# Setting up triangles between the steps of a state, and a modulation product on column quarters

## The chip, the cores and the metric

The kernel runs on one core of a Trainium2 chip. The metric is the device time of one execution in microseconds (us), lower is better. The engines are TensorE (PE; its weight loads are shown apart as PEld), VectorE (DVE), ScalarE (ACT), GpSimd (POOL) and SyncE (SP), which here issues all transfers between the device's memory and the cores' memory in one queue.

## The reference, cut to what matters

Two layers of a hybrid trunk over 2304 tokens (256 of context, 2048 latent) of 1024 channels. Each layer modulates a layer norm, projects it, runs three branches (a gated DeltaNet in both directions, a neighbourhood attention, a gated linear attention) and projects back.

```python
def ada_modulation(cond, w_mod, b_mod):
    h = (jax.nn.silu(cond) @ w_mod + b_mod)[..., None, :]
    return jnp.split(h, 3, axis=-1)
...
    amat = jnp.eye(c, dtype=F32) + lmat
    rhs = jnp.concatenate([v * beta[..., None], kb * jnp.exp(g)[..., None]], -1)
    sol = lax.linalg.triangular_solve(amat, rhs, left_side=True, lower=True, unit_diagonal=True)
...
    def step(s, inp):
        qk_i, qd_i, kd_i, u_i, w_i, gl_i = inp
        v_new = u_i - jnp.einsum('bhck,bhkv->bhcv', w_i, s)
        o = jnp.einsum('bhck,bhkv->bhcv', qd_i, s) + jnp.einsum('bhij,bhjv->bhiv', qk_i, v_new)
        s = s * gl_i[..., None, None] + jnp.einsum('bhck,bhcv->bhkv', kd_i, v_new)
        return s, o
```

The modulation has two rows (one for the latent tokens, one for the context) and 3072 columns per layer. The DeltaNet has four heads and two directions; its state is stepped chunk by chunk, and each chunk needs the inverse of a unit triangular matrix.

## The kernel before, in words

The program is written out in Python. A scheduler orders the instructions of each engine by priority, which is the order in which the program emits them: what is emitted first goes first when it is ready, and later work fills the gaps. The order is then fixed, and each engine runs its queue in order. Projections (`Dense`, L190) are three fp32r products per pair of blocks.

`stage_mod` (L90) computes the modulation in parts of 512 columns. For each part it loads eight tiles of weights of 128 x 512 (L102), multiplies them by the conditioning's two columns into a 2 x 512 output (L104), adds the bias (L105) and, for the first four parts, transposes the result into `modT` (L111, L112); the last two parts are the gate and go to `GT`. It runs in three places: at the very start (parts 0 to 3 of layer 0), inside layer 0 before the convolution of the DeltaNet's first two heads (parts 4 and 5 of layer 0 and 0 to 3 of layer 1), and at the same place in layer 1 (parts 4 and 5).

The DeltaNet works on chunks of 128 tokens, 18 of them; 3 chunks make a group. Heads go in pairs (`hp`, two of them), and the triangles of a pair are set up in three batches of two groups (`BATCHES`, six in all). For a batch there are three pieces of work:

- `prep` (L831): six chunks; each loads `kq` and `gb` (256 KB each), makes a product `pk` on TensorE (L849), and on DVE and ACT the triangle X and the matrix A (L853 to L860). The 32 x 32 diagonal blocks go out to device memory.
- `diagonal` (L879), with `invert` (L902): inverts 96 x 32-sized blocks on DVE: 30 rounds of one multiplication (L913) and one addition (L914).
- `solve` (L887), with `assemble` (L916): puts the inverse of the 128 x 128 triangles together with small TensorE products in five stages (L930, L936, L945, L956, L962).

`scan` (L966) steps the state: step n of both directions side by side. `step` (L978) has stages divided by `yield`: the product pk with the state (L999), R on DVE (L1003), pv (L1010), v on ACT (L1013), pd (L1017), the new state S on DVE (L1022), then the output po (L1030, L1032), which from the second visit of a chunk on is added to what the first visit stored (a load L1035, an addition L1036, a store L1040). A pair of heads has 18 steps, so a layer has 36, and they form one chain through the state.

The first batch is set up in `start`, between the convolutions of the two pairs. `run` emits the rest as a generator. Before its first `yield` stand prep(1), prep(2) and solve(0); then the layer emits the dense product for z (`dn.run(Wz, ...)`), and after it, up to the second `yield`, diagonal(1), solve(1), six steps, prep(3) and so on; each diagonal is emitted right before its solve. Then follow the attention of its first pair of heads (`na.pair`), the rest of `run`, and the attention of the second pair. So z's products have priority over all steps, and attention fills what the steps leave.

## Time and profile before

| | before |
|---|---|
| runs shown, median (lowest to highest) | 3989.75 us (3979.24 to 4000.7), 3 runs |
| profiled execution, its own time | 3995.01 us |
| its span, first to last instruction | 3992.9 us |
| mean granted TensorE clock | 0.913 |
| TensorE / DVE / ACT / POOL busy | 3626.0 / 2521.8 / 1660.0 / 810.2 us |
| bytes moved by DMA | 787.57 MB |

The profile comes from one execution of the program. A busy share is an average over stages that have different limits; a stage's own limit is read from a window of time, and a wait from the instruction that ended it.

### The profile page before, as it was taken

What the parts mean: (1) busy time and instruction counts of PE and PEld (TensorE: products, weight loads), DVE (VectorE), ACT (ScalarE), POOL (GpSimd) and SP (SyncE); (2) the same over time, 40 slices, a digit from 0 to 9 for tenths busy, and PEclk for the clock granted to TensorE, in tenths of its full rate; (3) what the DMA queues carried; (4) which work ended last, traced back from release to release, by engine and by line L of the source; (5) the groups of instructions that cost most, each with busy time, mean ns of one, the idle gap of its engine ahead of it and who ended that gap; (6) DMA issues with size and microseconds to landing.
All of it is one profiled execution on the core that took longest, in us unless ns stands there. A gap on an engine that the chain in (4) does not pass through costs nothing.

```text
span 3992.9 us, 77074 instructions
## 1 busy us (share of the span) xinstructions
PE 3626.0 (91%) x27262; PEld 3113.1 (78%) x27262; DVE 2521.8 (63%) x7471; ACT 1660.0 (42%) x4387; POOL 810.2 (20%) x1182
## 2 busy tenths in 40 slices
PE   7999998899989999897898999999999898989788
PEld 3777787579977888896676778887998788879676
DVE  5465462668975676356875556527798766753587
ACT  4533231335433454446545333213454244545342
POOL 0121111210101332221232211112111132331133
PEclk8988988899999998898898888899999998988899
DMA  9843435876687876666647443268776887775753
GB/s 312 280 147 105 133 112 169 245 232 201 205 276 219 246 229 189 187 196 214 203 132 232 152 147 115 100 210 251 215 232 201 285 228 205 228 217 150 219 160 111
DMA packets 756088, 787.57 MB, mean 197 GB/s; under 512 B 190207, under 2 KB 665207, under 8 KB 755703
## 3 DMA queue, kind: packets, MB, share of 16 engines
q1 hardware_dynamic: 755702, 782.64, 63.6%
q8 instruction: 216, 3.54, 0.4%
q14 instruction: 170, 1.38, 0.1%
HBM read 548.41 MB, written 234.03 MB: 196 GB/s over the span
## 4 chain that ended last, share of the span: by engine, by line
PE 55%; DMA 19%; DVE 16%; ACT 4%; issue 3%; SPq 2%; POOL 0%; DVEq 0%; ACTq 0%; POOLq 0%
PE p L190 29%; DMA mm<-MS 3%; PE p L1245 3%; DMA gb<-GR 2%; PE p L104 2%; DMA kk<-KK 2%; DMA raw<-in_w_in 1%; PE py L190 1%; PE po L1030 1%; PE pk L999 1%; PE pv L1010 1%; DMA oa<-OA 1%; PE pd L1017 1%; PE pt L1236 1%; DVE y L1374 1%
## 5 line engine op out<-in xcount | busy, mean ns | idle before, releaser
L190 PE MATMUL p<-mm,wh 128*128 128x384 f32 (+1 forms) x3648 | 1004.0, 354 | 67.2 <-DMA mm<-MS 21.4
L190 PEld LDWEIGHTS p<-mm,wh 128*128 128x128 f32 (+1 forms) x3648 | 667.8, 192 | 133.7 <-DMA mm<-MS 36.9
L190 PE MATMUL p<-mm,wl 128*128 128x384 f32 (+1 forms) x1824 | 635.1, 350 | 1.8 <-DVE wl L182 1.8
L190 PE MATMUL p<-wh,mm 128*128 128x512 f32 (+1 forms) x1696 | 570.5, 409 | 14.5 <-DMA mm<-MS 4.9
L190 PEld LDWEIGHTS p<-wh,mm 128*128 128x128 f32 x1696 | 329.1, 197 | 92.0 <-DMA mm<-MS 8.4
L649 DVE SCALAR_TENSOR_TENSOR acc<-pre,cw,acc 128x384 f32<-128x384 f32 (+1 forms) x576 | 351.8, 629 | 39.2 <-ACT acc L647 35.8
L190 PEld LDWEIGHTS p<-mm,wl 128*128 128x128 f32 (+1 forms) x1824 | 348.9, 191 | 22.8 <-issue 14.6
L190 PE MATMUL p<-wl,mm 128*128 128x512 f32 (+1 forms) x848 | 341.5, 403 | 4.3 <-DVE wl L182 4.3
L190 PE MATMUL py<-wh,mh 128*128 128x512 f32 x544 | 221.7, 410 | 17.1 <-ACT mh L1360 13.2
L190 PE MATMUL py<-wh,ml 128*128 128x512 f32 x544 | 213.9, 405 | 8.7 <-DVE ml L1361 8.7
L190 PE MATMUL py<-wl,mh 128*128 128x512 f32 x544 | 217.8, 402 | 0.0
L190 PEld LDWEIGHTS p<-wl,mm 128*128 128x128 f32 x848 | 166.5, 196 | 38.5 <-DVE wl L182 4.8
L992 POOL TENSOR_TENSOR kd<-kk,eD 128x256 f32<-128x256 f32 x144 | 90.4, 628 | 476.4 <-DMA kk<-KK 225.6
L1224 ACT ACTIVATE w<-w,mn 128x696 f32<-128x696 f32 (+2 forms) x136 | 112.9, 830 | 143.9 <-DVE mn L1221 142.6
L1383 POOL TENSOR_TENSOR y<-y,g 128x1024 f32<-128x1024 f32 x32 | 77.5, 2423 | 416.0 <-ACT y L1382 416.0
L639 POOL COPY pre<-pre 128x4 f32<-128x4 f32 x120 | 75.0, 627 | 416.4 <-DVE acc L649 244.1
L913 DVE TENSOR_TENSOR tmp<-M 96x30 f32<-96x30 f32 (+4 forms) x360 | 127.1, 353 | 27.7 <-issue 11.3
L1245 PE MATMUL p<-v,wl 120*128 120x64 f32 (+1 forms) x960 | 141.1, 286 | 0.0
L853 DVE SCALAR_TENSOR_TENSOR gb<-gb,Gt,mats 128x128 f32<-128x128 f32 x288 | 86.7, 358 | 83.0 <-DMA gb<-GR 82.8
L1261 DVE SCALAR_TENSOR_TENSOR zt<-zt,p 128x256 f32<-128x256 f32 (+1 forms) x102 | 51.4, 506 | 138.8 <-ACT zt L1260 131.9
L190 PEld LDWEIGHTS py<-wh,mh 128*128 128x128 f32 x544 | 106.4, 196 | 41.4 <-ACT mh L1360 16.1
L914 DVE TENSOR_TENSOR M<-M,tmp 96x30 f32<-96x30 f32 (+4 forms) x360 | 130.4, 362 | 6.1
(307 smaller groups left out, 8021.8 us busy)
## 6 DMA issues: line engine op xcount, KB each, us to landing
mm<-MS SPq DMA_DIRECT2D x384, 384.0 KB
kk<-KK SPq DMA_DIRECT2D x144, 512.0 KB
MS<-mm SPq DMA_DIRECT2D x96, 384.0 KB
raw<-in_w_in SPq DMA_DIRECT2D x104, 256.0 KB
w<-in_w_mod SPq DMA_DIRECT2D x96, 256.0 KB
M<-m SPq DMA_DIRECT2D x36, 512.0 KB
mm<-M SPq DMA_DIRECT2D x96, 192.0 KB
KK<-kq SPq DMA_DIRECT2D x96, 192.0 KB
```

The costliest lines, as they stand in the source:

```text
L104: nc.tensor.matmul(p, e.cc[:, k + j], w[:, j], start=k + j == 0, stop=k + j == KD - 1)
L190: e.nc.tensor.matmul(p, x(k), y(k), start=n == 0, stop=n == 3 * KD - 1)
L639: nc.gpsimd.tensor_copy(pre[:, 0:4], pre[:, m:m + 4])
L649: nc.vector.scalar_tensor_tensor(acc[:, :n], pre[:, k:k + n], w(kind, k), acc[:, :n], op0=ALU.mult, op1=ALU.add)
L853: nc.vector.scalar_tensor_tensor(E[:, d, h], gb[:, d, h], self.G[:, d, c, h0 + h:h0 + h + 1], e.mats[:, 1 + d], op0=ALU.subtract, op1=ALU.min)
L913: nc.vector.tensor_tensor(tv, col, row, op=ALU.mult)
L914: nc.vector.tensor_tensor(o, o, tv, op=ALU.add)
L992: nc.gpsimd.tensor_tensor(kd, kv[:, :, 0], self.eD[:, d, c, h0:h0 + 2].unsqueeze(2).to_broadcast([128, 2, 128]), op=ALU.mult)
L1224: nc.scalar.activation(w[:, a, 0:256 + nk], w[:, a, 0:256 + nk], AF.Exp, bias=m[:, a:a + 1], scale=-1.0, accum_out=sm[:, a:a + 1])
L1245: nc.tensor.matmul(p[:, a], l, r, start=j == 0, stop=j == len(parts) - 1)
L1261: nc.vector.scalar_tensor_tensor(th[:, :n], th[:, :n], 1.0, z, op0=ALU.add, op1=ALU.mult)
L1383: eng.tensor_tensor(y[:, s], y[:, s], self.g[:, 0, s], op=ALU.mult)
```

## The change

Two parts. `stage_mod` takes all its parts at once: for each of the eight slices of the contraction it loads tiles of 128 x 1024 weights (two parts), and the products of part i write to partitions 32i to 32i + 1 of one output bank, with the tile position (0, 32i), each part on its own quarter of the array's columns. Four bias additions follow, and four full transposes serve all parts.

The DeltaNet's `prep` and `diagonal` become generators with a `yield` after each chunk and each of the 30 rounds. `scan` takes such generators and, after each stage of a step but the first, runs `share // 6` of their parts, where `share` is 48 divided by the number of steps, rounded up: two parts for three steps, one for six. prep(2) now comes after the first three steps, and steps 0 to 2, diagonal(1) and prep(2) are emitted before the z product.

```diff
-def stage_mod(e, pool, ps, tag, tt, bufs, w_mod, b_mod, modT, GT, parts, step):
+def stage_mod(e, pool, ps, tag, tt, bufs, w_mod, b_mod, modT, GT, parts):
...
-        p = ps.tile([2, 512], F32, tag=tag, name="p")
-        for k in range(0, KD, step):
-            w = pool.tile([128, step, 512], F32, tag="wm", name="w", bufs=bufs)
-            nc.sync.dma_start(w, w4[:, k:k + step, s])
-            for j in range(step):
-                nc.tensor.matmul(p, e.cc[:, k + j], w[:, j], start=k + j == 0, stop=k + j == KD - 1)
-        nc.vector.tensor_tensor(b, b, p, op=ALU.add)
...
+    n0, n = parts[0], len(parts)
+    b = pool.tile([128, 512], F32, tag="bm", name="b", bufs=1)
+    nc.gpsimd.memset(b, 0.0)
+    for i, x in enumerate(parts):
+        nc.sync.dma_start(b[32 * i:32 * i + 2], b_mod[512 * x:512 * x + 512].partition_broadcast(2))
+    p = ps.tile([128, 512], F32, tag=tag, name="p")
+    for k in range(KD):
+        for i0 in range(0, n, 2):
+            w = pool.tile([128, 2, 512], F32, tag="wm", name="w", bufs=bufs)
+            nc.sync.dma_start(w, w4[:, k, 512 * (n0 + i0):512 * (n0 + i0) + 1024].rearrange("p (i c) -> p i c", i=2))
+            for i in range(i0, i0 + 2):
+                nc.tensor.matmul(p[32 * i:32 * i + 2], e.cc[:, k], w[:, i - i0], start=k == 0, stop=k == KD - 1, tile_position=(0, 32 * i))
+    for i in range(n):
+        r = slice(32 * i, 32 * i + 2)
+        nc.vector.tensor_tensor(b[r], b[r], p[r], op=ALU.add)
...
-        prep(1)
-        prep(2)
+        run = lambda *g: [None for x in g for _ in x]
+        run(prep(1))
         solve(0)
+        self.scan(self.st[0], range(3), diag(1))
+        run(prep(2))
         yield
-        for k in range(1, 6):
-            solve(k)
-            if k % 3:
-                self.scan(self.st[k // 3], range(6 * (k % 3) - 6, 6 * (k % 3)))
-            else:
-                self.scan(self.st[k // 3 - 1], range(12, 18))
-            prep(k + 2)
-            if k == 3:
-                yield
-        self.scan(self.st[1], range(12, 18))
+        solve(1)
+        self.scan(self.st[0], range(3, 6), diag(2))
+        solve(2)
+        self.scan(self.st[0], range(6, 12), prep(3), diag(3))
+        self.scan(self.st[0], range(12, 18), prep(4), diag(4))
+        yield
+        solve(3)
+        self.scan(self.st[1], range(3), prep(5))
+        solve(4)
+        self.scan(self.st[1], range(3, 6), diag(5))
+        solve(5)
+        self.scan(self.st[1], range(6, 18))
         yield
...
-    def scan(self, s, steps):
+    def scan(self, s, steps, *work):
+
         nc = self.e.nc
+        parts = (x for w in work for x in w)
+        share = -(-48 // len(steps))
...
-            for _ in zip(*both):
-                pass
+            for i, _ in enumerate(zip(*both)):
+                if i:
+                    for _ in range(share // 6):
+                        next(parts, None)
+        for _ in parts:
+            pass
```

At the start of layer 0 the order of emission changes too: the first block's loads of x come first, then one `stage_mod` of four parts with six buffers of 1024 columns in the place of eleven of 512; at the other two places two buffers in the place of four.

What the scheduler made of it, at three places. On TensorE at the second place of the modulation (L190, L198 after, is the projection's product; L104, L107 after, the modulation's), before:

```order
L104 MATMUL p<-w,cc 2x512
L190 MATMUL p<-mm,wl 128x384
L190 MATMUL p<-mm,wh 128x384
L104 MATMUL p<-w,cc 2x512
L190 MATMUL p<-mm,wh 128x384
L190 MATMUL p<-mm,wl 128x384
L190 MATMUL p<-mm,wh 128x384
L104 MATMUL p<-w,cc 2x512
```

and after:

```order
L198 MATMUL p<-mm,wh 128x384
L107 MATMUL p<-w,cc 2x512 x2
L198 MATMUL p<-mm,wh 128x384
L198 MATMUL p<-mm,wl 128x384
L198 MATMUL p<-mm,wh 128x384 x2
L198 MATMUL p<-mm,wl 128x384
L198 MATMUL p<-mm,wh 128x384
L107 MATMUL p<-w,cc 2x512 x2
```

Single products between the projection's became pairs.

On TensorE at the second step of the state in layer 0 (pk, pv, pd, po as above; L930 to L962 are solve), before:

```order
L956 MATMUL pz_13121<-t_13107,X 64x64 x6
L962 MATMUL px_13130<-X,z_13119 64x64 x6
L999 MATMUL pk<-S_13304,kk 128x128 x2
L1010 MATMUL pv<-R,X 128x128 x2
L962 MATMUL px_13138<-X,z_13128 64x64 x6
L930 MATMUL pz<-x_13012,X 32x32 x6
L930 MATMUL pz<-x_13011,X 32x32 x6
L1010 MATMUL pv<-R,X 128x128 x2
L1017 MATMUL pd<-v,kd 128x128 x2
```

and after (L1024, L1035, L1042 are pk, pv, pd; L980 solve; L864 prep; L198 the z product):

```order
L980 MATMUL px_12045<-X,z_12034 64x64 x6
L1024 MATMUL pk<-S_12102,kk 128x128 x2
L1035 MATMUL pv<-R,X 128x128 x2
L198 MATMUL p<-wh,mm 128x512 x2
L198 MATMUL p<-wl,mm 128x512
L198 MATMUL p<-wh,mm 128x512 x2
L198 MATMUL p<-wl,mm 128x512
L198 MATMUL p<-wh,mm 128x512 x2
L198 MATMUL p<-wl,mm 128x512
L198 MATMUL p<-wh,mm 128x512
L980 MATMUL px_12053<-X,z_12043 64x64 x6
L864 MATMUL pk<-kq 128x256 x2
```

Products of z moved in between the stages of the first steps. At the other end of layer 0, the last step and what follows it, before (L1229, L1236, L1245 are attention):

```order
L1010 MATMUL pv<-R,X 128x128 x2
L1229 MATMUL pt<-ident,w 128x128 x2
L1010 MATMUL pv<-R,X 128x128 x2
L1236 MATMUL pt<-ident,w 120x128 x2
L1236 MATMUL pt<-ident,w 80x128
L1017 MATMUL pd<-v,kd 128x128 x2
L1229 MATMUL pt<-ident,w 128x128 x2
L1017 MATMUL pd<-v,kd 128x128 x2
```

and after:

```order
L1024 MATMUL pk<-S_18390,kk 128x128 x2
L1024 MATMUL pk<-S_18393,kk 128x128 x2
L1035 MATMUL pv<-R,X 128x128 x4
L1042 MATMUL pd<-v,kd 128x128 x4
L1055 MATMUL po<-v,A 128x128
L1057 MATMUL po<-S_18390,kk 128x128
```

The last three steps of layer 0 have no attention beside them any more; in layer 1 they had none before either.

## Rows read from the trace of the kernel before

**Rows 1.** The page: busy time of each engine; the chain by engine.

```profile
PE 3626.0 (91%) x27262; PEld 3113.1 (78%) x27262; DVE 2521.8 (63%) x7471; ACT 1660.0 (42%) x4387; POOL 810.2 (20%) x1182
...
PE 55%; DMA 19%; DVE 16%; ACT 4%; issue 3%; SPq 2%; POOL 0%; DVEq 0%; ACTq 0%; POOLq 0%
```

**Rows 2.** Windows: span; us busy (count) of PE, PEld, DVE, ACT, POOL; clock; DMA share; GB/s.

```profile
0.00:45.00 45.00, 32.66 (x81) 6.14 (x81) 16.02 (x45) 5.05 (x10) 0.71 (x6) 1.00 0.94 307
715.00:870.00 155.00, 152.75 (x676) 101.63 (x677) 96.48 (x232) 51.97 (x131) 36.27 (x50) 0.98 0.88 254
1120.00:1220.00 100.00, 85.72 (x446) 67.81 (x445) 74.44 (x263) 30.42 (x82) 10.88 (x27) 0.88 0.99 320
1280.00:1340.00 60.00, 51.41 (x530) 45.82 (x529) 27.25 (x87) 23.85 (x68) 22.25 (x53) 0.91 0.95 255
1340.00:1690.00 350.00, 321.66 (x3118) 296.20 (x3118) 207.50 (x677) 174.22 (x479) 95.23 (x200) 0.89 0.72 206
1690.00:1790.00 100.00, 97.45 (x824) 94.65 (x823) 51.77 (x164) 53.99 (x150) 26.13 (x43) 1.00 0.68 205
2730.00:2780.00 50.00, 49.02 (x209) 31.50 (x210) 46.05 (x95) 21.02 (x47) 17.59 (x28) 0.97 0.97 279
3080.00:3180.00 100.00, 84.41 (x455) 66.23 (x454) 67.77 (x240) 30.36 (x81) 11.24 (x28) 0.89 1.01 331
```

**Rows 3.** TensorE around one product of the modulation (start, us); line L104 altogether.

```profile
754.13 1.02 PE L104 MATMUL p<-w,cc 128*2 128x512 f32 x2
...
755.08 0.45 PE L190 MATMUL p<-mm,wl 128*128 128x384 f32 x1
...
L104 PE MATMUL p<-w,cc x192: 591/592/1057, 9.4 to 2772.1; 128*2 128x512 f32 x192
```

**Rows 4.** TensorE where outputs lie in two halves (L486) and four quarters (L533).

```profile
600.55 0.27 PE L486 MATMUL pA<-a 32*64 32x64 f32 x2
...
629.60 0.39 PE L190 MATMUL p<-wl,mm 128*128 128x512 f32 x1
...
629.91 0.43 PE L533 MATMUL pS<-v,kd 128*32 128x64 f32 x16
...
630.27 0.74 PE L190 MATMUL p<-wh,mm 128*128 128x512 f32 x2
```

**Rows 5.** The chain, 0 to 50 us, in order of time (start, us, what).

```profile
30.20 5.23 DMA w<-in_w_mod
...
37.72 6.18 PE p L104 x14
...
43.92 0.67 DVE b L105
```

**Rows 6.** DVE waiting for gb: group, 1120 to 1220 us; total, times, longest, 1120 to 1800.

```profile
L853 DVE SCALAR_TENSOR_TENSOR gb<-gb,Gt,mats 128x128 f32<-128x128 f32 x51 | 14.5, 345 | 16.7 <-DMA gb<-GR 16.7
...
DVE gb L853 <- DMA gb<-GR: 44.7, 16, 7.0
```

**Rows 7.** The chain in late steps of layer 1, without attention.

```profile
3701.56 5.57 DMA OA<-o
...
3707.19 3.01 DMA o<-OA
...
3743.51 0.22 PE po L1030 x2
```

**Rows 8.** Groups of the whole span: one half of the rounds of inversion.

```profile
L914 DVE TENSOR_TENSOR M<-M,tmp 96x30 f32<-96x30 f32 (+4 forms) x360 | 130.4, 362 | 6.1
```

**Rows 9.** TensorE at pv of steps 3 and 6, and of three late ones, layer 0.

```profile
1298.53 0.71 PE L1010 MATMUL pv<-R,X 128*128 128x128 f32 x4
...
1337.47 0.71 PE L1010 MATMUL pv<-R,X 128*128 128x128 f32 x4
...
1754.37 1.05 PE L1010 MATMUL pv<-R,X 128*128 128x128 f32 x8
...
1775.37 1.05 PE L1010 MATMUL pv<-R,X 128*128 128x128 f32 x8
```

More of the change, by code (lines that the diff above doesn't have):

```diff
@@ new lines, in stage_mod @@
+    for i in range(n):
+        r = slice(32 * i, 32 * i + 2)
+        nc.vector.tensor_tensor(b[r], b[r], p[r], op=ALU.add)
+    if n0 >= 4:
+        for i in range(n):
+            nc.sync.dma_start(GT[:, 512 * (n0 - 4 + i):512 * (n0 - 3 + i)], b[32 * i:32 * i + 2])
+        return
+    pt = ps.tile([128, 4, 128], F32, tag=tt, name="pt")
+    for j in range(4):
+        nc.tensor.transpose(pt[:, j], b[:, j * 128:(j + 1) * 128], e.ident)
+    for i in range(n):
+        m = modT[:, 4 * (n0 + i):4 * (n0 + i) + 4]
+        nc.vector.tensor_scalar(m, pt[:, :, 32 * i:32 * i + 2], float(n0 + i >= 2), None, op0=ALU.add)
@@ L766, in start @@
         ax = lambda: [P.tile([128, 3, 2, 128], F32, tag=t, name=t) for t in "AX"]
-        self.XD[0] = self.prep(s, b, P, ps, "dn", ax)
-        self.diagonal(P, *self.XD[0])
+        for _ in self.prep(s, b, P, ps, "dn", ax, 0):
+            pass
+        for _ in self.diagonal(P, *self.XD[0]):
+            pass
     def weights(self, hp):
@@ L784, in prep, with diag @@
         def prep(k):
-            if k < len(self.BATCHES):
-                hp, b = self.BATCHES[k]
-                self.XD[k] = self.prep(self.st[hp], b, self.P1, self.ps, "pp", self.ax)
+            hp, b = self.BATCHES[k]
+            yield from self.prep(self.st[hp], b, self.P1, self.ps, "pp", self.ax, k)
+        def diag(k):
+            yield from self.diagonal(self.PM, *self.XD[k])
         def solve(k):
             hp, b = self.BATCHES[k]
-            if k:
-                self.diagonal(self.PM, *self.XD[k])
             self.solve(self.st[hp], b, *self.XD.pop(k))
@@ L829, in store, with prep @@
         self.e.nc.sync.dma_start(far["AX".index(t)], x.rearrange("p c h t -> p (c h t)"))
-    def prep(self, s, batch, P, ps, tag, ax):
+    def prep(self, s, batch, P, ps, tag, ax, key):
         e, nc = self.e, self.e.nc
@@ L860, in prep @@
                     nc.vector.tensor_tensor(A[d][:, ci], pk[:, :, 1], E[:, d], op=ALU.mult)
+                yield
             for d in range(2):
@@ L876, in prep @@
             nc.sync.dma_start(LD[b].rearrange("u j i -> j u i"), xd[32 * b:32 * b + 32].rearrange("p g u i -> p (g u) i"))
-        return n, LD, XD
+        self.XD[key] = n, LD, XD
+        yield
     def diagonal(self, P, n, LD, XD):
@@ L883, in diagonal @@
         nc.sync.dma_start(M, LD.rearrange("b u j i -> (b u) j i"))
-        self.invert(P, M, n)
+        yield from self.invert(P, M, n)
         nc.sync.dma_start(XD.rearrange("b u j i -> (b u) j i"), M)
@@ L914, in invert @@
             nc.vector.tensor_tensor(o, o, tv, op=ALU.add)
+            yield
     def assemble(self, X, d, xc, xt, i):
@@ L1428, in layer @@
                 p1 = stage_p1(e, P, ps, xsrc, layers[0].modT, M)
-                for n in (range(2), range(2, 4)):
-                    stage_mod(e, P, ps, "pa", "pm", 11, i["w_mod"][0], i["b_mod"][0], layers[0].modT, GT, n, 1)
-                    next(p1, None)
+                next(p1)
+                stage_mod(e, P, ps, "pa", "pm", 6, i["w_mod"][0], i["b_mod"][0], layers[0].modT, GT, range(4))
+                next(p1, None)
         def cbc(p, t):
@@ L1471, in layer @@
                                 if j < DEPTH:
-                                    stage_mod(e, P1, ps, "dn", "dn", 4, i["w_mod"][j], i["b_mod"][j], layers[j].modT, layers[j].GT, n, 1)
+                                    stage_mod(e, P1, ps, "dn", "dn", 2, i["w_mod"][j], i["b_mod"][j], layers[j].modT, layers[j].GT, n)
                             dn.run(W, gdn.conv(P, psh, 0) + gdn.conv(P, psh, 1), [], bufs=6, raws=4)
```

12 lines of the change are left out of this document (1 added, 11 removed).

## The prediction

> **What bounds the kernel now.** Start with the busy shares and the engines of the chain that ended last [rows 1]: TensorE (PE) is busy 91% of the span and carries 55% of the chain, DMA carries 19%, VectorE (DVE) 16%. So TensorE's instructions are the first currency: what leaves its queue counts where it has no gaps, and a wait counts where TensorE has nothing else to do. The stretches [rows 2] split that. From 715 to 870 us, where the modulation of the next layer runs between the convolution's products, TensorE is busy 152.75 of 155 us and DMA 0.88. At 2730 to 2780, the same place of layer 1, TensorE is full, but so are DVE (46.05 of 50) and DMA (0.97). From 1120 to 1220 and from 3080 to 3180, where triangles are set up before the state's steps, DMA is full (0.99 and 1.01) and TensorE idles 14.3 and 15.6 us. From 1690 to 1790, with attention between the steps, TensorE is full again. The first 45 us are a race of the weight transfers and the modulation's products.
>
> **Modulation on column quarters, second place (715 to 870 us).** One product of two rows is two instructions, since fp32 takes two passes; the row at 754.13 and the next one's start at 755.08 give 0.95 us from entry to exit [rows 3]. 48 of them take 48 x 0.95 = 45.6 us. After the change two products whose outputs lie in different quarters stand next to each other. That such pairs run at once is in the trace: two instructions on two 64-column halves take 0.27 us together, no more than one alone, and after 16 instructions on four quarters, which start at 629.91, the next full product starts at 630.27, 0.36 us later [rows 4]. One after another they would need more: the two instructions of a 512-column product start 1.02 - 0.59 = 0.43 us apart [rows 3], for 64 columns that is 0.054 us, and 16 of them 0.86 us. The order after has 22 adjacent pairs here and 4 products alone: 26 x 0.95 = 24.7 us, 20.9 less. I take 15 of it, since DMA at 0.88 must still bring the same weights and TensorE will wait for some; ends: 21 and nothing.
> The trace shows entering and leaving such a group as about 0.09 us on each side (629.60 to 629.91 where an undisturbed product takes 0.23, and before 630.27) [rows 4], and the 0.95 already holds that. The Trainium skill says in "TensorEngine Tiling (Array Packing)", Tiling Modes, Key Properties, that changing the tiling mode drains TensorE: this speaks against many small groups. If that came on top of a pair's 0.95, the 26 groups would pay 26 x 0.18 = 4.7 us and the gain would be 20.9 - 4.7 = 16.2; the trace agrees that there is a drain, but no run here shows whether a group of pairs pays more than a single product did.
>
> **Third place (2730 to 2780).** 16 products become 8 pairs: 8 x 0.95 = 7.6 us of TensorE, but DVE is busy 46 of 50 us there, so I take 2; ends 8 and 0.
>
> **First place (to 45 us).** 32 products become 16 pairs, so TensorE falls from bound to idle. But the chain there is transfers of weights (the last wait is 5.23 us) and then a tail of 14 instructions, 6.18 us [rows 5]. The new order loads three tiles of x first and more of the projection's weights before the last modulation tile: about 1.5 MB more, at the 307 GB/s of the stretch [rows 2] 4.9 us later; the tail shrinks from 6.2 to about 1.9 us (two pairs), and four bias additions (0.67 each [rows 5]) now follow each other where one stood, 2.0 us more. 4.9 - 4.3 + 2.0 = 2.6; the x tiles that came early save a little: I take +2, ends -4 and +6.
>
> **The triangles, a group ahead.** No work is added: the same 60 DVE instructions per diagonal (30 pairs at 2 x 0.36 = 0.72 us [rows 8], 21.7 us a diagonal), the same loads. Three things move.
> One: the second setting-up (`prep(2)`, 6 chunks with two loads of 256 KB each) leaves the crowded stretch. DVE waited for `gb` there 16.7 of the 100 us [rows 6], in twelve chunks; half of them go. I take 5 us per layer, 10 in all; ends: nothing, and all of the idle 14.3 + 15.6 = 29.9.
> Two: the first three steps of the state's chain now stand before the dense z product in the program, so that z's products fill them. In layer 0 the steps before came 13 us apart (four from 1298.5 to 1337.5 [rows 9]), while a step's own TensorE work is 20 products = 40 instructions of 0.11 us [rows 7], 4.4 us. The new order puts 48, 10 and 117 dense products around steps 2, 3 and 4 of layer 0, and 36, 45 and 87 in layer 1. Three steps at 13 - 4.4 give 26 us. In layer 1 less lay between them, so I take the late steps' 10 us (below): 3 x 5.6 = 17.
> Three: attention is used up earlier. Late steps take some 10 us with or without attention: three from 1754.4 to 1775.4 with it [rows 9], and without it the chain is the store and the load of the output tile, 5.57 + 3.01 us, then an addition and the next product [rows 7]. So attention there was free, and where it moves to it is not. From 1690 to 1790 TensorE is busy 97.45 us [rows 2]; ten steps take 44 of them, and the order has some 310 attention products there: 53 / 310 = 0.17 us each. In layer 0 some 105 such products move ahead of step 34: +18 us. In layer 1 the last steps were bare before, and some 32 move: +5.
> So layer 0: -26 + 18 = -8, layer 1: -17 + 5 = -12. Ends: without the first gain +18 and +5; without the second loss -26 and -17.
> The inversions wait for nothing new on their queue; what is queued behind them are R and S of the steps, at most one instruction of 0.36 us if they stay spread. The setting of the 128x512 bias tile to zero is four GpSimd instructions off any chain: POOL is busy 810 of 3993 us. Eight transposes stand in the place of 32 small ones: under 2 us in all, nothing.
>
> **Sum.** +2 - 15 - 2 - 10 - 8 - 12 = -45 us. Against the profiled execution's own 3995.0 us that is 3950; the median of the runs shown is 5.3 lower, 3989.75, so **3945 us**.
>
> **Rivals.**
> 1. Only the modulation counts: the steps' order is static, the same products stand in TensorE's queue, and what the steps gain under z is lost where attention is full. For it: TensorE busy 322 of 350 us between 1340 and 1690 [rows 2]. Then +2 - 15 - 2 = -15, 3975 us. Chance 0.25.
> 2. Slower: DVE becomes the chain of steps 2 to 6. Its queue is in order, and the order puts the whole of the first diagonal's 30 pairs and `prep(2)`'s `gb` additions in front of the first R and between the first S. If R and S are held by their share (two pairs a stage, six stages: 12 x 0.72 = 8.6 us a step) and by the loads of `gb` (up to 7.0 us [rows 6]), dense products in the queue are no cover, because their own evacuation is on DVE too. The 26 + 17 are gone, and the uncovered steps 5 and 6 of layer 0 and 5 of layer 1 cost 3 x 8.6 = 26: +2 - 15 - 2 - 10 + 18 + 5 + 26 = +24, 4014 us. It decides once steps 2 to 6 come more than 13 us apart again. Against it: DVE is busy 74 of 100 us in the crowded stretch and 208 of 350 us among the steps [rows 2]. Chance 0.13.
> 3. More than I sum: the granted clock is 0.88 at 1120 to 1220, 0.91 at 1280 to 1340 and 0.89 at 1340 to 1690 [rows 2], at 1.0 wherever TensorE has no gaps. Of the 350 us that last row leaves 0.11, 38 us of full speed, ungranted in a layer (the clock has two levels, 2.4 and 1.2 GHz). If the gaps close and a third of it comes back in both layers, 25 more, and 10 more of the idle: 3910 us. Chance 0.12.
> 4. It does not do what it says: the pairs do not overlap for two-row products, and the order moves nothing on the chain; then +2 and at most a few either way, 3990. Chance 0.05.
>
> **How the numbers follow.** The forecast has 0.45, its own ends about 3920 to 3972. About 0.5%, 20 us, is what a measurement of this kernel can tell from no change: below 3970 faster, above 4010 slower. Faster: nearly all of the forecast (0.41), a third of rival 1 (0.08), rival 3 (0.12): 0.61. Slower: two thirds of rival 2 and what is unforeseen, 0.13. Same: 0.26. The range 3900 to 4005 leaves out half of rival 2 and the far part of rival 3.
>
> **What would show it.** Right: pairs of the modulation's instructions starting within 0.01 us, its busy time about half of 96 x 0.95 = 91 us; TensorE idle in the setting-up stretch down by 5 us a layer; `gb` waits fewer; steps 2 to 4 between dense products; the last three steps of layer 0 bare, 10 us each. Wrong: TensorE waits for modulation weights at the second place; steps 2 to 6 of layer 0 over 13 us apart; a pause of attention products longer than before while the chain waits for the last diagonal.

## The result, and the profile after

The change made the kernel slower: 4038.1 us in the median of four runs (4026.1 to 4049.8) against 3990.9 before. The ratio on record is 1.0108 with a 95% interval of 1.0077 to 1.0139 (the two medians by themselves give 1.0118). The forecast was 3945 us, and the range ended at 4005. The profiled execution took 4030.25 us, its span is 4028.2.

The page of the kernel after, where [rows 1] stood before:

```profile
PE 3604.9 (89%) x27238; PEld 3130.5 (78%) x27238; DVE 2518.5 (63%) x7471; ACT 1658.3 (41%) x4387; POOL 819.0 (20%) x1186
...
PE 53%; DMA 20%; DVE 15%; ACT 5%; issue 3%; SPq 3%; POOL 1%; DVEq 0%; ACTq 0%; POOLq 0%
```

TensorE is busy 21 us less, in a span that is 35 us longer. So work was saved, and something else took more than it gave. To find where, compare the start of the same ACT, DVE and POOL instruction in both traces, in stretches of 40 us (median difference, after minus before; minus is earlier):

| at, before | what runs there | difference, us |
|---|---|---|
| 300 | first projections | -2 |
| 715 to 870 | second place of the modulation | -4, then -20 |
| 870 to 1120 | convolution of the second pair | -14, then -10 |
| 1800 | the states' steps of layer 0 are done | +15 |
| 2720 to 2800 | third place of the modulation | +11, then +4 |
| 3080 | convolutions of layer 1 are done | +9 |
| 3760 | the states' steps of layer 1 are done | +37 |

Everything is lost in two stretches, from the end of the convolutions to the start of the output projection. Here are both, first of the kernel before, windows with the columns of [rows 2], and ahead of them its second convolution:

```profile
870.00:1122.00 252.00, 248.86 (x1475) 244.13 (x1474) 218.10 (x726) 130.51 (x356) 27.70 (x58) 1.00 0.63 196
...
1122.00:1816.00 694.00, 619.60 (x5423) 555.47 (x5422) 400.80 (x1310) 307.55 (x851) 163.53 (x348) 0.91 0.76 227
3077.00:3767.00 690.00, 607.72 (x5266) 543.18 (x5267) 401.96 (x1300) 303.61 (x827) 164.42 (x344) 0.89 0.75 223
```

and the same two of the kernel after, with the places of the modulation, the crowded stretch of layer 0, a stretch in which the steps wait, the last steps, and the crowded stretch of layer 1:

```profile
0.00:45.00 45.00, 18.51 (x62) 1.51 (x64) 19.36 (x58) 6.47 (x14) 1.18 (x7) 0.89 0.95 323
711.00:851.00 140.00, 127.16 (x645) 101.08 (x644) 92.64 (x222) 51.77 (x131) 35.33 (x51) 0.93 0.93 261
...
1109.00:1209.00 100.00, 84.48 (x615) 69.41 (x614) 62.88 (x225) 32.34 (x90) 15.16 (x37) 0.86 0.90 295
1300.00:1360.00 60.00, 50.54 (x455) 44.70 (x453) 14.43 (x43) 25.36 (x71) 19.20 (x47) 0.69 0.61 168
1700.00:1800.00 100.00, 91.41 (x749) 87.35 (x747) 44.11 (x143) 45.46 (x129) 27.07 (x43) 0.95 0.71 210
...
3088.00:3188.00 100.00, 81.92 (x571) 65.45 (x570) 59.53 (x209) 29.69 (x83) 15.20 (x37) 0.90 0.90 298
...
1111.00:1833.00 722.00, 631.03 (x5423) 565.47 (x5421) 403.49 (x1323) 313.26 (x860) 164.00 (x348) 0.88 0.74 220
3086.00:3804.00 718.00, 624.75 (x5266) 560.47 (x5265) 398.11 (x1299) 301.55 (x827) 163.58 (x344) 0.86 0.72 214
```

As many TensorE instructions, 5423, took 694 us and then 722, and 5266 took 690 and then 718: 28 us more in each layer. No engine has more to do: the counts of VectorE and ScalarE are the same within about 1%. TensorE is idle 91 us where it was idle 74 (722 - 631 and 694 - 620), and its granted clock is 0.88 for 0.91. Taking the ungranted part off (631.0 - 0.12 x 722 = 544 after, 619.6 - 0.09 x 694 = 557 before; an estimate, as if TensorE were busy in all of it), the products themselves did not become longer. A stretch in which idle time and slow clock grow and the work does not is not set by that work: it waits for a chain.

Which chain? The triangles, and the last batch above all. The last products of the last `solve` (the 64 x 64 ones, L962 before and L980 after), group of the line in the stretch, the time after "to" being the last start. Before, layers 0 and 1:

```profile
L962 PE MATMUL px<-X,z x48: 218/218/267, 1660.4 to 1682.1; 64*64 64x64 f32 x48
...
L962 PE MATMUL px<-X,z x48: 218/289/366, 3613.3 to 3639.3; 64*64 64x64 f32 x48
```

After:

```profile
L980 PE MATMUL px<-X,z x96: 218/218/366, 1604.7 to 1706.1; 64*64 64x64 f32 x96
...
L980 PE MATMUL px<-X,z x48: 218/289/366, 3655.5 to 3679.9; 64*64 64x64 f32 x48
```

Counted from the last addition of the convolution (at 1122 and 3077 before, 1111 and 3086 after) the last solve ends at 560 and 562 us before, and at 595 and 594 after. From there to the first product of the output projection it is 134 and 127 us before, 127 and 124 after.

And where does it fall behind? The ends of the solves of layer 0, from the end of the convolution: before 136, 180, 256, 366, 472, 560; after 106, 185, 258, 448, 516, 595. The first comes 30 us earlier, the third at the same time, the fourth, which is the first of the second pair, 82 us later; the two solves behind it make up 47 of these 82. The three pieces of this batch show why, each the group of its line in the stretch: the products of prep(3), the rounds of diagonal(3), the first products of solve(3). Before:

```profile
L849 PE MATMUL pk<-kq x24: 378/379/483, 1301.5 to 1334.4; 128*128 128x256 f32 x24
...
L913 DVE TENSOR_TENSOR tmp<-M x30: 149/363/595, 1366.8 to 1426.9; 96x30 f32<-96x30 f32 x2, 96x58 f32<-96x58 f32 x2, 96x84 f32<-96x84 f32 x2, 96x108 f32<-96x108 f32 x2
...
L930 PE MATMUL pz<-x,X x96: 191/191/212, 1444.5 to 1474.4; 32*32 32x32 f32 x96
```

After:

```profile
L864 PE MATMUL pk<-kq x24: 379/379/483, 1368.8 to 1382.3; 128*128 128x256 f32 x24
...
L930 DVE TENSOR_TENSOR tmp<-M x30: 151/350/707, 1417.7 to 1488.6; 96x30 f32<-96x30 f32 x2, 96x58 f32<-96x58 f32 x2, 96x84 f32<-96x84 f32 x2, 96x108 f32<-96x108 f32 x2
...
L948 PE MATMUL pz<-x,X x96: 191/191/212, 1513.2 to 1543.5; 32*32 32x32 f32 x96
```

By the clock of the whole trace, the lateness is there with the first piece, 67 us, and the two behind it keep it: 51 us at the diagonal, 69 at the solve.

Before, prep(3) was emitted behind the first six steps and ahead of solve(2), and ran ahead of it. The change hands it out to steps 6 to 11, which are emitted behind solve(2), and the first of its products starts where solve(2) ends (1369 us). That solve had waited for its own diagonal, and the steps for it: the R instructions of the steps (the first step has none) come at 1208, 1233, 1274, 1292, 1300, 1313, and then at 1366. The diagonal was put a group ahead of its solve; the setting-up of the second pair was put a solve behind.

What held prep(3) was not its input: the loads of its first two `kq` tiles had been issued at 1234 and 1243 us. Its products follow the last product of the solve that is emitted ahead of it. On TensorE before (solve(1), then prep(3)):

```profile
1300.65 0.91 PE L962 MATMUL px<-X,z 64*64 64x64 f32 x12
1301.49 1.13 PE L849 MATMUL pk<-kq 128*128 128x256 f32 x4
```

and after (solve(2), then prep(3)):

```profile
1368.00 0.91 PE L980 MATMUL px<-X,z 64*64 64x64 f32 x12
1368.84 1.99 PE L864 MATMUL pk<-kq 128*128 128x256 f32 x8
```

In all 18 kernels of the table below, in both layers, the first product of prep(3) starts within 1 us of the end of the solve emitted ahead of it: solve(1) in ten kernels, solve(2) in eight. So the place in the program was more than a priority here. The program offers a reason: prep's `pk` and the outputs of `assemble` are tiles of one tag, `pp`, which has three banks. That the shared banks are what holds prep(3) was not tried.

### The profile page after: what moved, and what is told of

It is laid out like the page before. It is cut to its first block, busy times and chain, and to the rows that moved or that the text cites. A ratio compares the mean times of both kernels' runs of the same rounds, so it can differ in the third digit from the quotient of the medians.

```text
span 4028.2 us, 76863 instructions
## 1 busy us (share of the span) xinstructions
PE 3604.9 (89%) x27238; PEld 3130.5 (78%) x27238; DVE 2518.5 (63%) x7471; ACT 1658.3 (41%) x4387; POOL 819.0 (20%) x1186
## 4 chain that ended last, share of the span: by engine, by line
PE 53%; DMA 20%; DVE 15%; ACT 5%; issue 3%; SPq 3%; POOL 1%; DVEq 0%; ACTq 0%; POOLq 0%
PE p L198 28%; DMA mm<-MS 4%; PE p L1270 3%; DMA gb<-GR 2%; DMA raw<-in_w_in 2%; PE py L198 2%; DMA mm<-M 1%; DMA OA<-o 1%; PE pv L1035 1%; DMA oa<-OA 1%; PE pd L1042 1%; DVE mix L1375 1%; DVE mix L1376 1%; PE po L1055 1%; PE pA L494 1%
## 5 line engine op out<-in xcount | busy, mean ns | idle before, releaser
L198 PE MATMUL p<-mm,wh 128*128 128x384 f32 (+1 forms) x3648 | 997.6, 353 | 78.0 <-DMA mm<-MS 28.3
L198 PEld LDWEIGHTS p<-mm,wh 128*128 128x128 f32 (+1 forms) x3648 | 666.4, 192 | 135.3 <-DMA mm<-MS 42.0
L198 PE MATMUL p<-mm,wl 128*128 128x384 f32 (+1 forms) x1824 | 630.4, 348 | 1.7 <-DVE wl L190 1.7
L198 PE MATMUL p<-wh,mm 128*128 128x512 f32 (+1 forms) x1696 | 568.4, 408 | 27.8 <-DMA mm<-MS 12.6
L198 PEld LDWEIGHTS p<-wh,mm 128*128 128x128 f32 x1696 | 330.4, 197 | 104.7 <-DMA mm<-MS 16.0
L198 PEld LDWEIGHTS p<-mm,wl 128*128 128x128 f32 (+1 forms) x1824 | 348.6, 191 | 14.9 <-issue 7.1
L198 PE MATMUL p<-wl,mm 128*128 128x512 f32 (+1 forms) x848 | 344.7, 406 | 4.3 <-DVE wl L190 4.3
L198 PE MATMUL py<-wh,mh 128*128 128x512 f32 x544 | 222.7, 411 | 22.4 <-ACT mh L1385 18.4
L198 PE MATMUL py<-wh,ml 128*128 128x512 f32 x544 | 215.0, 408 | 14.0 <-DVE ml L1386 14.0
L198 PE MATMUL py<-wl,mh 128*128 128x512 f32 x544 | 219.0, 404 | 0.0
L198 PEld LDWEIGHTS p<-wl,mm 128*128 128x128 f32 x848 | 167.3, 197 | 38.7 <-DVE wl L190 4.8
L930 DVE TENSOR_TENSOR tmp<-M 96x30 f32<-96x30 f32 (+4 forms) x360 | 126.3, 351 | 53.4 <-issue 41.5
L1038 ACT ACTIVATE v<-pv,Wt 128x128 f32<-128x128 f32 x288 | 87.9, 365 | 149.9 <-PE pv L1035 149.3
L198 PEld LDWEIGHTS py<-wh,mh 128*128 128x128 f32 x544 | 106.9, 197 | 46.3 <-ACT mh L1385 21.1
L1270 PEld LDWEIGHTS p<-v,wl 120*128 120x128 f32 (+1 forms) x960 | 138.1, 214 | 0.6
L198 PEld LDWEIGHTS py<-wh,ml 128*128 128x128 f32 x544 | 106.6, 196 | 39.5 <-DVE ml L1386 17.7
```

The lines of the kernel that those rows point to most:

```text
L198: e.nc.tensor.matmul(p, x(k), y(k), start=n == 0, stop=n == 3 * KD - 1)
L930: nc.vector.tensor_tensor(tv, col, row, op=ALU.mult)
L1038: nc.scalar.activation(v[:, h], pv[:, h], AF.Copy, scale=sc(self.W, h))
L1270: nc.tensor.matmul(p[:, a], l, r, start=j == 0, stop=j == len(parts) - 1)
```

## The experiments

All times are medians. The kernel before had 3990.9 us beside the change and 3997 to 3999 us beside the other runs, and each ratio is against the kernel before beside the same runs; where a run is set against the change, the ratios are the fairer comparison. "Last solve" is the end of the last solve in layers 0 and 1, counted from the end of the convolution, and "stretch" the time from there to the output projection, both from the trace of one execution, which lies up to 22 us off the median (mod_first more, see below).

| run | time, us | ratio (95%) | last solve | stretch |
|---|---|---|---|---|
| before | 3990.9 | 1 | 560, 562 | 694, 690 |
| the change | 4038.1 | 1.0108 (1.0077 to 1.0139) | 595, 594 | 722, 718 |
| mod_only | 4017.4 | 1.0048 (1.0025 to 1.0070) | 554, 578 | 692, 709 |
| tri_only | 4083.6 | 1.0205 (1.0173 to 1.0238) | 637, 604 | 763, 735 |
| first3 | 3990.5 | 0.9983 (0.9961 to 1.0005) | 556, 550 | 697, 682 |
| late_part | 4029.3 | 1.0086 (1.0059 to 1.0112) | 590, 586 | 725, 719 |
| solve3_early | 4148.9 | 1.0384 (1.0342 to 1.0425) | 657, 624 | 779, 736 |
| no_spread | 4068.5 | 1.0159 (1.0121 to 1.0197) | 637, 581 | 761, 706 |
| mod_first | 3987.7 | 0.9989 (0.9958 to 1.0019) | (575, 571) | (712, 704) |
| first3_old | 3987.1 | 0.9978 (0.9952 to 1.0004) | 547, 558 | 682, 690 |
| less_attention | 4018.7 | 1.0051 (1.0029 to 1.0074) | 597, 569 | 717, 688 |
| few_rounds | 3952.3 | 0.9878 (0.9853 to 0.9903) | 529, 555 | 669, 687 |
| ahead1 | 3998.9 | 0.9988 (0.9967 to 1.0009) | 577, 551 | 715, 681 |
| ahead3 | 4029.8 | 1.0074 (1.0051 to 1.0097) | 569, 565 | 710, 698 |
| prep3_early | 3998.7 | 1.0002 (0.9979 to 1.0025) | 562, 551 | 704, 680 |
| as_before_handed | 3988.6 | 0.9980 (0.9957 to 1.0003) | 551, 571 | 693, 704 |
| o3_after | 4075.3 | 1.0193 (1.0164 to 1.0221) | 609, 588 | 745, 715 |
| o3_first3_old | 3982.8 | 0.9957 (0.9932 to 0.9981) | 548, 544 | 687, 668 |

The trace of mod_first is of an execution that took 4035.9 us where the median is 3987.7, so its numbers stand in brackets.

### The two parts alone

mod_only: the kernel before with the `stage_mod` of the change at its three places.

```diff
-def stage_mod(e, pool, ps, tag, tt, bufs, w_mod, b_mod, modT, GT, parts, step):
+def stage_mod(e, pool, ps, tag, tt, bufs, w_mod, b_mod, modT, GT, parts):
```

> The kernel before with the new modulation alone. Every theory that puts the loss into the triangles expects here what the two traces show up to the end of the second convolution and around the third place: the kernel after is 11 us ahead at 1111 us and gains 2 to 3 more at 2850, so 3991 - 13 = 3978 us (3970 to 3985). The rival, that the pairs bring nothing by themselves and that those 13 us are the luck of one profiled execution, expects 3991.

tri_only: the change with that function and its three places as before.

```diff
-def stage_mod(e, pool, ps, tag, tt, bufs, w_mod, b_mod, modT, GT, parts):
+def stage_mod(e, pool, ps, tag, tt, bufs, w_mod, b_mod, modT, GT, parts, step):
```

> The change with the old modulation. If the two parts only add, the modulation's 13 us are missing: 4038 + 13 = 4051 us. If the new modulation also hurts later (its 8 us of slow clock right behind it, from 870 to 1122 us), less: about 4040.

Both missed. The modulation alone took 4017 us, not 3978, although it does what it should: the convolution ends at 1109 us. Its stretch of layer 1 took 709 us where before had 690, with nothing changed in that part of the program. The triangles alone cost 86 us, the modulation alone 20, both together 47. The parts don't add. The scheduler orders everything behind an edit anew: of TensorE's instructions among the steps, only some 60% stand in mod_only in the order that they have before (the longest series that keeps its order, in either layer). That this is why they don't add was not tried.

### The front part and the back part

first3 undoes the change from step 3 on:

```diff
-        self.scan(self.st[0], range(3, 6), diag(2))
+        self.scan(self.st[0], range(3, 6))
+        run(prep(3), diag(2))
         solve(2)
-        self.scan(self.st[0], range(6, 12), prep(3), diag(3))
-        self.scan(self.st[0], range(12, 18), prep(4), diag(4))
-        yield
+        self.scan(self.st[0], range(6, 12))
+        run(prep(4), diag(3))
         solve(3)
+        self.scan(self.st[0], range(12, 18))
...
```

> New modulation, and of the triangles only the front part: steps 0 to 2 with diagonal(1), then prep(2), stand ahead of the z product; from step 3 on the order of emission is that of before, with nothing handed out. Theory ORDER (the loss comes from behind: the second pair is set up later, solve(3) behind step 17, so the last solve ends later and the steps behind it run bare) expects the front gain of some 20 us to stay: 3978 - 20 = 3958 us. Theory CLOCK (z's dense products no longer stand between the small products of the solves, so that these run in clumps at the lower clock, some 36 us more of it in each layer) expects the loss to be here already: 3978 + 2 x 15 = 4008 us. Theory HAND-OUT (rounds of inversion stand in front of R and S of the steps) expects most of the loss to be gone, about 3975 us.

late_part undoes the front and keeps the rest:

```diff
         run(prep(1))
+        run(prep(2))
         solve(0)
-        self.scan(self.st[0], range(3), diag(1))
-        run(prep(2))
         yield
+        run(diag(1))
         solve(1)
-        self.scan(self.st[0], range(3, 6), diag(2))
+        self.scan(self.st[0], range(6), diag(2))
```

> New modulation, the start as before (both preps, solve(0), then z, then diagonal(1) at once, solve(1), and six steps with diagonal(2) handed out), and from solve(2) on the order of the change. Theory ORDER expects the whole loss and no front gain: 4038 + 10 = 4048 us or more. Theory CLOCK expects z back between the solves and the loss gone: about 3985 us. Theory HAND-OUT expects two thirds of the loss: 3978 + 40 = 4018 us.

The loss is in the back part: late_part has stretches of 725 and 719 us, as the change has, and first3 has 697 and 682. No theory had both times: ORDER, which puts the loss there, wanted 3958 and 4048 us or more, and HAND-OUT 3975 and 4018. CLOCK, as stated, falls with that: bringing z back between the solves did not bring the loss down, and taking it away in first3 cost nothing. first3 stands 27 us under mod_only, but late_part, without the front, is no slower than the change; so a gain of the front is not shown on its own.

### Order or handing out

solve3_early moves one line, no_spread takes the handing out away:

```diff
         self.scan(self.st[0], range(6, 12), prep(3), diag(3))
+        solve(3)
         self.scan(self.st[0], range(12, 18), prep(4), diag(4))
         yield
-        solve(3)
```

> The change with one line moved: solve(3) ahead of steps 12 to 17 of the first pair, where it stood before, and not behind them. Theory ORDER (the back part of the new order sets up the second pair later; in the profile of the change solve(3) begins at 1513 us, before at 1445) expects most of the loss behind step 6 to go, some 20 us a layer: about 4000 us. Theory HAND-OUT (the loss behind step 6 comes from rounds and chunks between the stages of the steps) expects no change, 4038 us. Theory RESHUFFLE (any edit gives another order of the scheduler with its own waits, and its luck is worth 20 us in either direction) expects anything from 4010 to 4060 us.

```diff
             for i, _ in enumerate(zip(*both)):
-                if i:
-                    for _ in range(share // 6):
-                        next(parts, None)
+                pass
```

> The change with the same order of pieces, but prep and diagonal are emitted at once behind the steps that they were handed out to. Theory HAND-OUT expects the loss of the back part to be gone: about 3990 us, as with the front part alone. Theory ORDER expects it to stay or to grow, since prep(3) and diagonal(3) come later still: 4040 to 4055 us. Theory RESHUFFLE: 4010 to 4060 us.

Without handing out the time is no shorter than with it, so HAND-OUT falls: it is 30 us longer by the medians and 0.5% by the ratios, whose intervals overlap. solve3_early missed in the other direction, 4149 us. Its solve(3) ends at 1523 us, 36 earlier than in the change, but prep(4) now comes behind it (from 1523, against 1395), two steps behind it lie 93 us apart, and the last solve ends at 1765. So the place of solve(3) by itself is not the cause; the time follows the last solve here too. In the change solve(3) had also come to stand behind the second `yield`, and so behind the attention of the first pair of heads; prep3_early, below, leaves it there.

### Whether the modulation's first place or the old modulation matters

mod_first has the new `stage_mod` at the first place alone, first3_old is first3 with the old one everywhere.

> The kernel before with the new modulation at the first place alone; the other two places and the triangles are as before. The traces of the change show its own effect as 1 to 3 us by 300 us. If nothing else mattered: 3997 - 2 = 3995 us. Theory RESHUFFLE expects the states' stretches to differ by 10 us or more in at least one layer, although nothing was changed there, and so 3985 or 4010 us.

> The front part of the triangles alone with the old modulation. If the front part's gain over the new modulation alone (4017 - 3990 = 27 us) is its own, 3997 - 27 = 3970 us. If the two parts disturb each other (the change without the new modulation took 4084, with it 4038), the front part gives nothing here: 3990 to 4010 us. Theory CLOCK (the first steps take z's dense products away from the solves) expects more slow clock in the states' stretches than before, and 4010 us or more.

mod_first stands 9 us under before and first3_old 10, both with intervals that hold 1. The new modulation gave +20 us on before (mod_only), +3 on the front part (first3 against first3_old) and -46 on the whole change (against tri_only; about -39 by the ratios). An effect whose sign depends on what stands behind it is not that of the modulation: it gains some 11 us by the end of the convolution, in the mean of the kernels that have it throughout (1106 to 1119 us, against 1120 to 1125 in those that have it not), and that is less than what another order of the steps is worth.

### What the stretch is made of

Both start from the change. less_attention takes products from TensorE, few_rounds takes rounds from VectorE.

```diff
-[(wl[a][:k, j], v[:k, j, c]) for j, (_, k) in enumerate(chunks)]
+[(wl[a][:k, j], v[:k, j, c]) for j, (_, k) in enumerate(chunks) if j < 1]
```

> The change, with part of attention's work on TensorE left out: of the products of the local weights with v only the first chunk of each row is computed, so 704 of 960 instructions of 0.295 us (row of the profile of the change), up to 108 us of TensorE over the two layers. Theory TENSORE (what my prediction started from: in the states' stretches the products in TensorE's queue are what the time is made of) expects 60 to 100 us less, 3940 to 3980 us. Theory CHAIN (a layer's stretch ends some 100 us behind its last solve, whatever else is in the queue, and the solves follow each other by prep, diagonal and solve) expects 4020 to 4050 us: the products were filling waits.

```diff
-        for k in range(1, 31):
+        for k in range(1, 31, 3):
```

> The change, with 10 of the 30 rounds of each inversion (every third), so the triangles are not inverted. VectorE loses two thirds of its rounds, TensorE's products are all there. Theory CHAIN expects the diagonals on the way to the last solve, 71 + 37 us in layer 0, to shrink to a third and the last solve to end 40 to 70 us earlier in each layer: 3900 to 3960 us. Theory TENSORE expects the same time as with all rounds, since VectorE is no bound: 4025 to 4040 us.

The two pages' first lines, less_attention:

```profile
PE 3530.3 (88%) x26534; PEld 3046.8 (76%) x26534; DVE 2523.7 (63%) x7471; ACT 1661.0 (41%) x4387; POOL 807.6 (20%) x1186
```

few_rounds:

```profile
PE 3578.2 (91%) x27238; PEld 3103.4 (79%) x27238; DVE 2365.2 (60%) x6991; ACT 1657.1 (42%) x4387; POOL 802.4 (20%) x1186
```

704 products less and 75 us less TensorE: 19 us less time, 23 by the ratios, and a last solve that is 25 us earlier in layer 1. 480 VectorE instructions less, 153 us of an engine that is busy 63%: 86 us less time, 92 by the ratios. This is the sharpest pair of the study, though an edit also makes a new order, which alone may be worth some 20 us (mod_only). In few_rounds the same 27238 instructions kept TensorE busy 27 us less, at a mean granted clock of 0.911 in place of 0.901, so part of its gain is clock. The last solve of few_rounds, layer 0:

```profile
L980 PE MATMUL px<-X,z x48: 218/218/267, 1623.3 to 1644.5; 64*64 64x64 f32 x48
```

It ends 529 us behind the convolution, 66 less than in the change; in layer 1 it is 39 less.

### Priority ahead of the steps

ahead1 and ahead3 start from first3 and emit `prep`, `diagonal` and `solve` three steps earlier; ahead3 puts solve(4) ahead of step 12 and prep(5) behind step 17.

```diff
         solve(2)
-        self.scan(self.st[0], range(6, 12))
-        run(prep(4), diag(3))
+        run(diag(3))
+        self.scan(self.st[0], range(6, 9))
+        run(prep(4))
         solve(3)
...
```

> New modulation, front part of the change, nothing handed out; behind it prep, diagonal and solve of a batch stand ahead of the steps in emission, three steps earlier than before. Theory CHAIN expects the last solve to end earlier than with the front part alone (1665 and 3618 us in that profile), and 3960 to 3980 us if it does by 10 us or more a layer; if the tiles for A and X are what prep(5) waits for, the last solve stays where it is, and so does the time: 3990 us. Theory TENSORE expects 3990 us.

> As the run before, but solve(4) ahead of steps 12 to 17 of the first pair, and prep(5) behind them. Theory CHAIN: the time follows the end of the last solve; if prep(5) is late because it must wait for the tiles of steps 12 to 17, that is later than with the front part alone and the time is 3990 us or more; else 3970 us. Theory TENSORE expects 3990 us.

No gain, and CHAIN's 3960 to 3980 us missed: in ahead1 the last solve ends at 577 and 551 us, in first3 at 556 and 550. In ahead3 prep(5) starts at 1540 us, behind solve(4), where first3 has it at 1470, and the time is 39 us longer than first3's, some 20 of it in the last output projection (248 us, first3 230), which no theory had named. Its prep(5) starts within 1 us of the end of solve(4), which is emitted ahead of it, as prep(3) does above. Whether the tiles for A and X also hold prep(5) back was not tried.

### The place of prep(3)

prep3_early is the change with prep(3) at the place of before; as_before_handed restores the places of prep(4) and solve(3) too, and still hands out the diagonals.

```diff
         self.scan(self.st[0], range(3, 6), diag(2))
+        run(prep(3))
         solve(2)
-        self.scan(self.st[0], range(6, 12), prep(3), diag(3))
+        self.scan(self.st[0], range(6, 12), diag(3))
```

> The change with prep(3) ahead of solve(2), emitted at once, and diagonal(3) alone handed out to steps 6 to 11; all else is the change. If the place of prep(3) is the cause, the last solve ends some 30 us earlier in each layer (565 in place of 595 us behind the convolutions) and the time is 3985 to 4000 us. If the handing out is the cause, it stays at 4030 to 4040 us.

> The change with the places of before for the first pair's second half (prep(3) ahead of solve(2), prep(4) ahead of solve(3), solve(3) ahead of steps 12 to 17), and the diagonals 2, 3 and 4 still handed out; the second pair as in the change. If the places are the cause: 3985 to 4000 us, and no more than the run before. If the handing out delays diagonals (71 us for diagonal(3) in the change, 61 before): 4010 us or more.

Both as the place of prep(3) would have it. In prep3_early, products of prep(3) and the last ones of the last solve in layer 0:

```profile
L865 PE MATMUL pk<-kq x24: 379/379/634, 1301.8 to 1332.4; 128*128 128x256 f32 x24
...
L981 PE MATMUL px<-X,z x48: 218/218/267, 1659.6 to 1680.8; 64*64 64x64 f32 x48
```

prep(3) is back at 1302 us, the last solve ends at 562 and 551 us, and the whole loss is gone, 3999 us. Handing out the diagonals costs nothing (3989). Both runs also emit prep(3) at once; that this alone is not the gain is shown by no_spread, which emits it at once behind the six steps and is no faster than the change. In the ten kernels that have prep(3) ahead of solve(2), the last solve ends 544 to 578 us behind the convolution; in the six with all rounds and all products that have it behind, 581 to 657.

### The stretch behind the last solve

A third output tile, in the change and in first3_old:

```diff
-        ot = t("o", 2)
+        ot = t("o", 3)
```

> The change with three tiles in place of two for the output of a step, so that a load need not wait for the store of the step before. If the 100 us behind the last solve are the chain of store and load (5.57 + 3.01 us of each 10 us), 12 steps lose 1 to 3 us each, and the time falls by 20 to 70 us, to 3970 to 4020 us, the less, the more attention is left for that stretch. If they are TensorE's work, nothing: 4038 us.

> The front part of the triangles with the old modulation (3987 us) and three output tiles. If the stretch behind the last solve is that chain: 3930 to 3970 us. If it is TensorE's work, since more attention is left there (114 of 240 products with v in layer 0, 84 in the change): 3987 us.

The queue's waits in the last steps of layer 1 (total, times, longest), first the change, then o3_after:

```profile
SPq L1060 <- DMA OA<-o: 24.7, 12, 4.5
```

```profile
SPq L1060 <- DMA OA<-o: 24.4, 10, 5.0
```

The third tile did not take the wait away: the load of an output still waits for a store. The stretch from the last solve to the output projection stays (136 and 127 us, where the change has 127 and 124), so this run does not tell a chain from TensorE's work there, and both forecasts missed. That o3_after is 37 us slower goes with its last solve in layer 0, 609 us. o3_first3_old is the one kernel with all its work that is faster than before beyond its interval, 0.9957 (0.9932 to 0.9981); it is not clear of first3_old (0.9952 to 1.0004). Since the tile did not do what it was to do, I take its order for the reason (last solve at 548 and 544) and not the tile; that is not shown.

## Why the prediction was wrong

**The premise.** "TensorE's instructions are the first currency" holds for the convolutions, where the new modulation brought its gain. Among the steps it does not. In 36 stretches (18 kernels, two layers) the time from the last solve to the output projection is 131 us on average, 112 to 142; what stands before it runs from 529 to 657, and the length of the stretch follows that with a correlation of 0.97. It holds that time as its larger part, so the correlation says little by itself; what counts is that the rest hardly varies, and that two edits moved the last solve and the time with it, shorter inversions (few_rounds) and the place of prep(3) (prep3_early). Taking 75 us off TensorE gave 19, shortening the inversions gave 86.

**The modulation.** First place: taken +2, found -2 by 300 us; TensorE had half the work to do (18.5 us busy in place of 32.7) and idled for it. Second place: taken -15 with 20.9 as the most, found -16 by its end, as [rows 3, 4] had it. One row shows two products, four instructions, in the time of one, and a wait for weights ahead of them:

```profile
744.61 1.03 PE L107 MATMUL p<-w,cc 128*2 128x512 f32 x4 [0.81 <-DMA w<-in_w_mod]
```

Of the 16 us some 6 were left at the end of the second convolution. Third place: taken -2, found -8, of which 5 were given back by the end of the convolutions. The sizes were about right where they act, and all that was left of them is some 13 us.

**prep(2) out of the crowded stretch.** I took -10 for both layers from DVE's waits for `gb`. They fell from 44.7 us [rows 6] to:

```profile
DVE gb L868 <- DMA gb<-GR: 27.6, 20, 3.8
```

and the first solve ended 30 us earlier. One sign that I had named did not come: TensorE idled 15.5 of the first 100 us in place of 14.3 [rows 2], and 18.1 in place of 15.6 in layer 1. And solve(2) ended at 258 us, before at 256. What is gained ahead of a batch that waits for something else is not gained at the end.

**The steps under z (-26 and -17), and what I left out beside them.** This is the step that failed. I counted steps of 13 us [rows 9] that z would cover, along the state's chain. The first steps did come earlier (the first R of layer 0 by 77 us, the sixth by 37), as the order had shown. But the one behind the sixth came 53 us behind it, with solve(2) in between, and of the 37 us that the sixth was early it kept 7. Among the "three things" that move, the second pair's setting-up was missing: prep(3) behind solve(2) stood in the sum at nothing, under "the inversions wait for nothing new on their queue". It put the fourth solve 82 us and the last one 35 us later (32 in layer 1), and the stretches of the two layers, summed as -8 and -12, became 28 us longer each. With prep(3) back in its place the loss is gone (prep3_early). I costed the diagonals as work ("21.7 us a diagonal") and never as a date: of a piece that moves I asked what it collides with, and not who waits for its last result. The diff holds it already: prep(3) is handed to steps 6 to 11, one line below solve(2).

**Attention (+18 and +5).** I priced its products at 0.17 us each, as if a product moved were a product added to the end. The last three steps of layer 0 did come bare, and took what late steps took before ([rows 9]: three from 1754 to 1775; after, R at 1784, 1796, 1804). From the last solve to the output projection it is no longer than before: there was no such loss.

**The rivals.** Rival 2 had the sign and half the size of the loss (+24 us, 4014), by the wrong mechanism: VectorE's rounds in front of R and S. Handing them out costs nothing (as_before_handed), and emitting them at once gains nothing (no_spread). Its sign to look for, steps 2 to 6 more than 13 us apart, did appear, 25 and 41 us among them. But the R behind the 41 us, at 1274 us, waited for its product pk, which TensorE began at 1272.6, behind products of z and of solve(1). Rival 3 looked for more granted clock; there was less, 0.88 and 0.86 in the two stretches. Its premise, a clock of 1.0 wherever TensorE has no gaps, is a little more than [rows 2] show: 0.97 and 0.98 in two stretches that are 98% busy or more. Rival 4, pairs that do not overlap, falls with the row at 744.61. Rival 1, that only the modulation counts, did not come true even with the modulation alone (4017 us).

**Still open.** How much of one kernel's 20 us against another is the luck of a new order. mod_only lost them in stretches that it did not touch, and no run here held the order fixed.

## What to carry to other kernels

Before costing a reordering by busy time, find the last result that the end of the stage waits for and list the pieces that it is made of with their times; a piece that moves behind another of that list can cost much of its delay (here 35 of 82 us in layer 0), even when the engine that it feeds is busy 63%, and work taken off an engine that is 90% full may gain little (here 19 us for 75). "Handed out between steps" is also "not before those steps": put only such work there as has a step to spare. Where a scheduler orders anew behind every edit, compare the parts of a change at the place where they act; at the end, an effect of a few tenths of a per cent can carry either sign.

## What the runs showed of the hardware

The granted clock of TensorE was 1.00 at 870 to 1122 us before, where the convolutions keep it busy 248.9 of 252 us. It was 0.69 at 1300 to 1360 us in the kernel after, where it is busy 50.5 of 60 us, for the most part with products of attention and with the small ones of solve(2) (32 x 32 and 64 x 64). In steps of 10 us: from 1300 to 1320 TensorE was busy 6.1 and 5.6 us; from 1320 to 1340 it was busy 9.5 and 10.0 us, but at a granted clock of 0.50, the lower of its two levels (1.2 in place of 2.4 GHz); at 1350 to 1360 it was back at 1.00. So this stretch, in which the steps wait for triangles, pays twice: in idle time, and with what runs behind it at the lower level. I had counted on the clock as a gain (rival 3) and not as a price of waiting.
